# A hybrid encoder trunk: the 96 columns of the small projections become a unit of their own, the gate units get 512 columns

## The chip, the cores and the metric

The kernel runs on one core of one Trainium2 chip. The metric is the device time in microseconds (us) of one execution. Engines are named as the profile names them: PE is TensorE's matmul side and PEld its weight loads, DVE is VectorE, ACT is ScalarE, POOL is GpSimd, SP is SyncE, which issues the transfers.

## The reference

Two layers over 256 tokens of 1024 features, all in float32. What matters here is the input projection of the mixer in the middle of each layer, one matrix of 6752 columns that is cut among all branches:

```python
h = rms_norm(x, mix_norm[l])
z = h @ w_in[l]
(na_q, na_k, na_v, gq, gk, gv, gr, gfl, gbl, c_q, c_kv, k_rope, gates) = split_cols(z, IN_SPLITS)
...
gt = jax.nn.sigmoid(gates.reshape(B, S, N_BRANCH, D))
mixed = (gt[:, :, 0] * (y_na @ w_br_na[l])
         + gt[:, :, 1] * (y_gla @ w_br_gla[l])
         + gt[:, :, 2] * (y_mla @ w_br_mla[l]))
x = x + mixed @ w_out[l]
```

`gates` has 3 x 1024 columns, one set for each branch. Three small parts, `k_rope` (64 columns, the rotary key), `gfl` and `gbl` (16 each, the low-rank decays), have 96 columns together. Around the mixer stand two feed-forward blocks with 2816 inner features.

## The kernel before, in words

The 256 tokens are two tiles of 128 (t = 0, 1). The normalised input lies transposed in `xT`, as the stationary operand of the projections. Every float32 product is made of three matmuls in the type float32r: each operand is split into a high part (hi) and a rest (lo), and `burst` (L372) issues hi x hi, hi x lo and lo x hi for each block k of 128 input features. The product goes through the helper `mm` (L370 in the profile), so the profile has one line for nearly all matmuls, each with a weight load of its own on PEld.

Weights come in *units*, a list (L85 on) in the order of use; a unit is a transfer of up to 128 x 2048 values into one of three `raw` buffers (SP's queue). ACT copies it in two halves to the hi part of an `hl` buffer (L143), DVE subtracts to get the lo part (L149); after the second lo half of unit j the transfer of unit j+3 is issued. `unit()` (L162) hands out the next unit and sees that its halves, and the first of the one after, are in the queues; `tick()` (L186) is called between bursts, splits ahead by up to two units, and moves the side tasks (attention, linear attention) a step on.

`dense8(N, evac)` (L389) is one projection of N columns: two units of four k blocks each, for each unit both token tiles with 12 matmuls of N columns, then the eviction `evac` of each tile's accumulator. So N columns cost 48 matmuls, whatever N is. The order in a mixer is: `m` (latent q and kv), `gr`, then `dense8(512, ev_r)` (L1132), then `v` with the bursts of the unit `uq` (384 columns) between, `q`, `gv`, `k`, the two linear-attention projections, four times `dense8(GATEN, ev_g(g))` (L1162), the two late gate units, the branch products and the output product.

The step with `ev_r` is called the *small-projection step* below. Its 512 columns are the 96 of the small parts and the first 416 of the gates (GATE0). `ev_r` (L622) evicts a tile: DVE scales the 96 columns into `rl` (L624) and copies a part of them (L625), ACT copies the 416 gate columns into `gates` (L627) and sums the squares of 64 columns (L629). The four steps with `ev_g`, the *gate step*, hold the next 4 x 408 gate columns (GATEN), which ACT copies into `gates` (L634). The sigmoid is applied later, in place.

```python
def dense8(N, evac, pre=None, between=None):
    ...
    accs = [acc_t(), acc_t()]
    for kh in range(2):
        u = unit()
        for t in range(2):
            ...
            burst(accs[t][:, :N], X, u, range(4 * kh, 4 * kh + 4), t, N, kh == 0, kh == 1)
```

Of the kernel before, what the change touches and what calls it, by code (L numbers as in the profile page):

```python
# [10 lines left out]
AF = mybir.ActivationFunctionType  # L11
# [7 lines left out]
NCH = DFF // 256  # L19
NB = DFF // 128  # L20
EPS = 1e-6
GATE0 = 416
GATEN = 408

SPLIT_AHEAD = 2
RAW_BUFS = 3
# [20 lines left out]
def body(tc, T):  # L47
# [3 lines left out]
    with ctx:  # L51
# [24 lines left out]
        for l in range(DEPTH):  # L76
            W = T["layers"][l]
            for kh in range(2 if l else 0):
                units.append((W["f1_up"][kh], 2048))
            for c in range(2 if l else 0, NB):  # L80
                units.append((W["f1_w13"][c], 2048))
            for u in range(NCH):
                units.append((W["f1_w2"][u], 2048))
            def add(nm):
                for kh in range(2):  # L85
                    units.append((W["in_" + nm][kh], 2048))

            add("m")
            add("gr")
            add("r")  # L90
            units.append((W["uq"], 1536))
            add("nv")
            add("nq")
            units.append((W["ukv"], 2048))
            add("gv")
            add("nk")
            for j in range(2):
                units.append((W["in_qk"][j], 2048))
            for g in range(4):
                for kh in range(2):  # L100
                    units.append((W["in_g"][g, kh], 4 * GATEN))
            for h in range(2):
                for kh in range(2):
                    units.append((W["in_late"][h, kh], 2048))
            for b in ("na", "mla", "gla"):
                for h in range(2):
                    units.append((W["br_" + b][h], 2048))
            for u in range(4):
                units.append((W["out"][u], 2048))
            for kh in range(2):  # L110
                units.append((W["f2_up"][kh], 2048))
            for c in range(2, NB):
                units.append((W["f2_w13"][c], 2048))
            for u in range(NCH):
                units.append((W["f2_w2"][u], 2048))
# [273 lines left out]
        def dense8(N, evac, pre=None, between=None):  # L389
            tks = []  # L390
            if pre is not None:
                ua, ub = unit(), unit()
                for t in range(2):
                    for h in range(2):
                        finish(pre[t, h])
                    acc = acc_t()
                    burst(acc[:, :N], X, ua, range(4), t, N, True, False)
                    tick(t == 0)
                    burst(acc[:, :N], X, ub, range(4, 8), t, N, False, True)
                    tks.append(drain(evac, t, acc))  # L400
                    tick()
                return tks
# [4 lines that stand above are left out]
                    if kh == 0 and between:  # L407
                        between(t)
                    burst(accs[t][:, :N], X, u, range(4 * kh, 4 * kh + 4), t, N, kh == 0, kh == 1)
                    if kh:  # L410
                        tks.append(drain(evac, t, accs[t]))
                    tick()
            return tks
# [150 lines left out]
        def mixer(l, norms, after, prefetch):  # L564
# [57 lines left out]
            def ev_r(t, acc):  # L622
                r = rl[t] = small(160, tag="rl", bufs=2)
                DVE.tensor_scalar(r[:, :96], acc[:, :96], rs_x[t], None, op0=ALU.mult)  # L624
                DVE.tensor_copy(r[:, 96:].rearrange("p (q n) -> p q n", q=2),  # L625
                                r[:, None, 64:96].to_broadcast([128, 2, 32]))
                ACT.activation(out=gates[:, t, :GATE0], in_=acc[:, 96:512], func=AF.Copy, scale=rs_x[t])  # L627
                ssr[t] = small(1)
                ACT.activation(out=junk(64), in_=r[:, :64], func=AF.Square, accum_out=ssr[t])  # L629

            def ev_g(g):
                def f(t, acc):
                    a = GATE0 + g * GATEN
                    ACT.activation(out=gates[:, t, a:a + GATEN], in_=acc[:, :GATEN], func=AF.Copy, scale=rs_x[t])  # L634
                return f

# [492 lines left out]
            c_tk = spawn(c_task(m_tk), 1)  # L1129
            dense8(512, ev_gr)  # L1130
            rs_bcast()
            dense8(512, ev_r)  # L1132
            prefetch()
            finish(c_tk)
            u_tk = []
# [124 lines left out]
def _tok(a):  # L1260
    return np.ascontiguousarray(a)
# [37 lines left out]
def layout(inp):  # L1299
    A = {}  # L1300
    A["x"] = _tok(inp["x"].reshape(SEQ, D))
    xT = inp["x"].reshape(SEQ, 8, 128).transpose(2, 1, 0)
    A["gcol"] = _tok(inp["ffn1_norm"][0].reshape(8, 128).T)
    A["ident"] = np.eye(128, dtype=np.float32)
    A["rope"] = _rope()
    j, i = np.arange(128)[:, None], np.arange(128)[None, :]
    A["am"] = _tok((j % 64 > i)[:, :64].astype(np.int32))
    dr, dc, ok = _rel_index()
    for l in range(DEPTH):
        p = f"l{l}_"  # L1310
        for f in ("1", "2"):
            w1, w3, w2 = (inp[f"ffn{f}_w{n}"][l] for n in (1, 3, 2))
            a = np.stack([w.reshape(8, 128, NB, 128).transpose(2, 1, 0, 3) for w in (w1, w3)], 3)
            A[p + f"f{f}_w13"] = _tok(a.reshape(NB, 128, 2048))
            if (l, f) == (0, "1"):
                A["first"] = _tok(np.concatenate([xT] + [a[c].reshape(128, 8, 256) for c in range(FIRST_R)], 2))
            else:
                A[p + f"f{f}_up"] = _tok(a[:2].reshape(2, 128, 2, 4, 256).transpose(2, 1, 3, 0, 4).reshape(2, 128, 2048))
            A[p + f"f{f}_w2"] = _kt(w2, 2)
            A[p + f"g{f}"] = _tok(inp[f"ffn{f}_norm"][l].reshape(8, 128).T)  # L1320
        A[p + "gm"] = _tok(inp["mix_norm"][l].reshape(8, 128).T)
        w = inp["w_in"][l]
        sizes = (("nq", 512), ("nk", 512), ("nv", 512), ("gq", 256), ("gk", 256), ("gv", 512), ("gr", 512),
                 ("gfl", 16), ("gbl", 16), ("cq", 256), ("ckv", 256), ("kr", 64), ("gates", 3072))
        part, o = {}, 0
        for nme, n in sizes:
            part[nme] = w[:, o:o + n]
            o += n
        g = part["gates"]
        g = np.concatenate([g[:, :1024], g[:, 2048:], g[:, 1024:2048]], 1)  # L1330
        A[p + "in_gr"] = _k4(part["gr"])
        A[p + "in_m"] = _k4(np.concatenate([part["cq"], part["ckv"]], 1))
        A[p + "in_r"] = _k4(np.concatenate([part["kr"], part["gfl"], part["gbl"], g[:, :GATE0]], 1))
        for nme in ("nq", "nk", "nv", "gv"):
            A[p + "in_" + nme] = _k4(part[nme])
        A[p + "in_qk"] = _tok(np.stack([_kt(part["gq"], 8)[0], _kt(part["gk"], 8)[0]]))
        A[p + "in_g"] = _tok(np.stack([_k4(g[:, GATE0 + i * GATEN:GATE0 + (i + 1) * GATEN]) for i in range(4)]))
        A[p + "in_late"] = _tok(np.stack([_k4(g[:, 2048 + h * 512:2048 + (h + 1) * 512]) for h in range(2)]))
        A[p + "uq"] = _kt(inp["mla_w_uq"][l], 2)[0]
        A[p + "ukv"] = _kt(inp["mla_w_ukv"][l], 2)[0]  # L1340
        for b in ("na", "gla", "mla"):
            wb = inp["w_br_" + b][l]
            A[p + "br_" + b] = _tok(np.stack([_kt(wb[:, h * 512:(h + 1) * 512], 4)[0] for h in range(2)]))
        A[p + "out"] = _kt(inp["w_out"][l], 2)
        A[p + "row"] = np.concatenate([inp["gla_out_norm"][l], inp["mla_q_norm"][l], inp["mla_k_norm"][l],
                                       inp["mla_cq_norm"][l], inp["mla_ckv_norm"][l]])
        col = np.zeros((128, COLN), np.float32)
        col[:, 0] = np.tile(inp["na_q_norm"][l], 2)
        col[:, 1] = np.tile(inp["na_k_norm"][l], 2)
        col[:, 2:4] = inp["gla_gf_bias"][l].reshape(2, 128).T  # L1350
        col[:, 4:6] = inp["gla_gb_bias"][l].reshape(2, 128).T
        A[p + "col"] = col
        gup = np.zeros((32, 512), np.float32)
        gup[:16, :256] = inp["gla_gf_up"][l]
        gup[16:, 256:] = inp["gla_gb_up"][l]
        A[p + "gup"] = gup
        b = np.where(ok[None], inp["na_rpb"][l][:, dr, dc], np.float32(-1e30)).astype(np.float32)
        A[p + "bias"] = _tok(b.reshape(4, 2, 2, 128, 128).transpose(0, 3, 1, 2, 4))
    return A
# [23 lines left out]
```

## Time and profile before

| what | value |
|---|---|
| median of 3 runs | 1239.62 us (1239.03 to 1239.73) |
| the profiled execution | 1239.52 us |
| its span, first to last instruction | 1237.7 us |
| PE busy | 1233.5 us, 100% of the span |
| DVE busy | 892.4 us, 72% |
| ACT busy | 710.9 us, 57% |
| mean granted TensorE clock | 1.000 |

The profile is of one execution, and 1.8 us of its time lie around the span. Matmuls are pipelined: a recorded matmul of 512 columns lasts 0.39 us, while the next one starts 0.23 us after it. A pace is therefore read from a chain or from a row that merges many, and not from the mean of one. A row that merges equal instructions gives the time from the start of the first to the end of the last.

### The profile page before, as it was taken

The numbers are of one execution on the slowest core, as the hardware profiler recorded it, in microseconds if no ns is written. First come the engines' busy times: TensorE is split into PE (matmuls) and PEld (weight loads), VectorE is DVE, ScalarE is ACT, GpSimd is POOL, SyncE is SP. The second block draws the span as 40 slices with busy tenths as digits, with TensorE's granted clock in tenths as the row PEclk, the third lists the DMA queues.
The fourth block names the chain that finished last, engine by engine and source line by source line (L and its number), as shares of the span: only waits on it lengthen the run. The fifth ranks groups of instructions, "written<-read, shape, count | busy, mean of one in ns | idle before, by whom it ended". The sixth has DMA issues, their size and how long they took to land.

```text
span 1237.7 us, 18188 instructions
## 1 busy us (share of the span) xinstructions
PE 1233.5 (100%) x7048; PEld 1061.4 (86%) x7048; DVE 892.4 (72%) x1399; ACT 710.9 (57%) x1317; POOL 217.6 (18%) x165
## 2 busy tenths in 40 slices
PE   9999999999999999999999999999999999999999
PEld 8888888889988888888888888888899888888887
DVE  6888837689667778886478886476896677788862
ACT  7665536567755465655356565356686654656541
POOL 0222102132112012220012220021322030122200
PEclk9999999999999999999999999999999999999999
DMA  8655744662554455557355556346525445555560
GB/s 332 211 202 177 252 150 162 224 195 93 187 190 146 173 200 178 201 177 249 119 204 207 191 195 247 108 172 238 176 99 201 171 142 190 188 195 189 186 238 34
DMA packets 37910, 228.58 MB, mean 185 GB/s; under 512 B 5760, under 2 KB 7040, under 8 KB 13376
## 3 DMA queue, kind: packets, MB, share of 16 engines
q1 hardware_dynamic: 37680, 227.42, 52.0%
q8 instruction: 55, 0.90, 0.3%
q14 instruction: 31, 0.25, 0.1%
q10 hardware_dynamic: 144, 0.00, 0.0%
HBM read 224.26 MB, written 1.05 MB: 182 GB/s over the span
## 4 chain that ended last, share of the span: by engine, by line
PE 100%; DVE 0%; issue 0%
PE acc L370 81%; PE ta L370 16%; PE ta L699 1%; PE ta L264 1%; PE ta L308 0%; PE ta L1211 0%; PE ta L684 0%; PE ta L737 0%; PE ta L616 0%; PE ta L1026 0%; PE ta L299 0%; PE ta L477 0%; PE ta L956 0%; DVE x L554 0%; DVE junk L305 0%
## 5 line engine op out<-in xcount | busy, mean ns | idle before, releaser
L149 DVE TENSOR_TENSOR hl<-raw,hl 128x1024 fp32r<-128x1024 f32 (+1 forms) x418 | 561.2, 1383 | 83.6 <-ACT hl L143 73.2
L143 ACT ACTIVATE hl<-raw 128x1024 fp32r<-128x1024 f32 (+1 forms) x418 | 412.8, 1040 | 103.4 <-PE ta L370 81.3
L370 PE MATMUL acc<-xT,hl 128*128 128x256 f32 (+1 forms) x2720 | 464.7, 332 | 0.0
L370 PEld LDWEIGHTS acc<-xT,hl 128*128 128x128 f32 x2720 | 407.6, 188 | 54.7
L370 PE MATMUL acc<-hl,xT 128*128 128x512 f32 (+1 forms) x1584 | 362.1, 384 | 0.0
L370 PEld LDWEIGHTS acc<-hl,xT 128*128 128x128 f32 x1584 | 291.9, 188 | 47.7 <-issue 1.7
L370 PE MATMUL acc<-hl,s 128*128 128x512 f32 x816 | 193.6, 390 | 0.0
L370 PEld LDWEIGHTS acc<-hl,s 128*128 128x128 f32 x816 | 152.5, 188 | 31.7 <-issue 0.3
L491 POOL TENSOR_TENSOR s<-s,rsb 128x512 f32<-128x512 f32 x79 | 109.5, 1387 | 352.4 <-DVE s L490 352.4
L370 PE MATMUL ta<-hl,s 128*128 128x512 f32 (+2 forms) x648 | 148.3, 378 | 0.0
L370 PEld LDWEIGHTS ta<-hl,s 128*128 128x128 f32 x648 | 117.6, 188 | 21.7
L500 ACT ACTIVATE s<-s 128x256 fp32r<-128x256 f32 x82 | 34.0, 417 | 168.2 <-DVE s L498 168.2
L490 DVE TENSOR_TENSOR s<-acc,s 128x256 f32<-128x256 f32 x158 | 59.7, 420 | 58.4 <-ACT s L489 58.4
L577 POOL TENSOR_TENSOR sm<-sm,mhalf 128x4 f32<-128x4 f32 (+2 forms) x24 | 36.7, 1531 | 192.0 <-DVE sm L581 192.0
L285 POOL TENSOR_TENSOR sm<-sm,mhalf 128x1 f32<-128x1 f32 x12 | 14.1, 1176 | 294.3 <-DVE sm L284 294.3
L489 ACT ACTIVATE s<-acc 128x256 f32<-128x256 f32 x158 | 50.6, 372 | 0.0
L248 DVE TENSOR_TENSOR s<-ta,s 128x512 fp32r<-128x512 f32 (+1 forms) x46 | 26.6, 604 | 30.0 <-ACT s L247 29.9
L267 ACT ACTIVATE xT<-ta,gain 128x128 fp32r<-128x128 f32 x80 | 22.8, 368 | 36.3 <-PE ta L264 36.3
L247 ACT ACTIVATE s<-ta 128x512 fp32r<-128x512 f32 (+1 forms) x46 | 22.9, 532 | 31.4 <-PE ta L699 16.9
L496 ACT ACTIVATE s<-s 128x256 f32<-128x256 f32 x82 | 34.2, 419 | 11.3 <-POOL s L491 0.3
L370 PE MATMUL ta<-s,s 64*64 64x128 f32 (+4 forms) x720 | 35.8, 260 | 0.0
L370 PEld LDWEIGHTS ta<-s,s 64*64 64x64 f32 (+3 forms) x720 | 30.4, 145 | 5.9 <-issue 4.2
(164 smaller groups left out, 676.6 us busy)
## 6 DMA issues: line engine op xcount, KB each, us to landing
raw<-in_l_f_w SPq DMA_DIRECT2D x123, 1024.0 KB, 4.8
raw<-in_l_in_g SPq DMA_DIRECT2D x16, 816.0 KB, 4.4
raw<-in_l_in_late SPq DMA_DIRECT2D x8, 1024.0 KB, 4.8
raw<-in_l_out SPq DMA_DIRECT2D x8, 1024.0 KB, 4.7
raw<-in_l_f_up SPq DMA_DIRECT2D x6, 1024.0 KB, 4.8
raw<-in_l_in_m SPq DMA_DIRECT2D x4, 1024.0 KB, 4.8
raw<-in_l_in_gr SPq DMA_DIRECT2D x4, 1024.0 KB, 4.8
raw<-in_l_in_r SPq DMA_DIRECT2D x4, 1024.0 KB, 4.8
```

Of the source, the lines that this page charges most:

```text
L143: ACT.activation(out=hls[j][:, 0, sl], in_=raws[j][:, sl], func=AF.Copy)
L149: DVE.tensor_tensor(out=hl[:, 1, sl], in0=r[:, sl], in1=hl[:, 0, sl].bitcast(F32), op=ALU.subtract)
L247: ACT.activation(out=hi, in_=ps, func=AF.Copy)
L248: DVE.tensor_tensor(out=lo, in0=ps, in1=hi.bitcast(F32), op=ALU.subtract)
L267: ACT.activation(out=xT[:, t, 0, kk, :], in_=ps[:, k * 128:(k + 1) * 128], func=AF.Copy, scale=G[:, kk:kk + 1])
L370: PE.matmul(out=out, lhsT=lhsT, rhs=rhs, start=start, stop=stop, skip_group_check=True)
L489: ACT.activation(out=g[:, j, :], in_=a[j][:, 256:], func=AF.Copy)
L490: DVE.tensor_tensor(out=g[:, j, :], in0=a[j][:, :256], in1=g[:, j, :], op=ALU.add)
L491: POOL.tensor_tensor(out=g, in0=g, in1=rb[:, None, :].to_broadcast([128, 2, 256]), op=ALU.mult)
L496: ACT.activation(out=g[:, 0, :], in_=g[:, 0, :], func=AF.Silu)
L500: ACT.activation(out=o[:, 0, :], in_=g[:, 0, :], func=AF.Copy)
L577: POOL.tensor_tensor(out=r[:, :n], in0=ss[:, :n], in1=mhalf[:, :n], op=ALU.pow)
```

## The change

The 96 columns get one unit of 768 values a partition (8 blocks of 96), used in one burst of 24 matmuls for each token tile. The first 2048 gate columns come in four steps of 512 columns instead of 416 and 4 x 408. There is one unit fewer in a layer.

```diff
--- before.py
+++ after.py
@@ -19,8 +19,7 @@
 NCH = DFF // 256
 NB = DFF // 128
 EPS = 1e-6
-GATE0 = 416
-GATEN = 408
+GATEN = 512
 
 SPLIT_AHEAD = 2
 RAW_BUFS = 3
@@ -87,7 +86,7 @@
 
             add("m")
             add("gr")
-            add("r")
+            units.append((W["in_r"], 768))
             units.append((W["uq"], 1536))
             add("nv")
             add("nq")
@@ -624,13 +623,12 @@
                 DVE.tensor_scalar(r[:, :96], acc[:, :96], rs_x[t], None, op0=ALU.mult)
                 DVE.tensor_copy(r[:, 96:].rearrange("p (q n) -> p q n", q=2),
                                 r[:, None, 64:96].to_broadcast([128, 2, 32]))
-                ACT.activation(out=gates[:, t, :GATE0], in_=acc[:, 96:512], func=AF.Copy, scale=rs_x[t])
                 ssr[t] = small(1)
                 ACT.activation(out=junk(64), in_=r[:, :64], func=AF.Square, accum_out=ssr[t])
 
             def ev_g(g):
                 def f(t, acc):
-                    a = GATE0 + g * GATEN
+                    a = g * GATEN
                     ACT.activation(out=gates[:, t, a:a + GATEN], in_=acc[:, :GATEN], func=AF.Copy, scale=rs_x[t])
                 return f
 
@@ -1129,7 +1127,12 @@
             c_tk = spawn(c_task(m_tk), 1)
             dense8(512, ev_gr)
             rs_bcast()
-            dense8(512, ev_r)
+            hl = unit()
+            for t in range(2):
+                acc = acc_t()
+                burst(acc[:, :96], X, hl, range(8), t, 96, True, True)
+                ev_r(t, acc)
+                tick()
             prefetch()
             finish(c_tk)
             u_tk = []
@@ -1330,11 +1333,11 @@
         g = np.concatenate([g[:, :1024], g[:, 2048:], g[:, 1024:2048]], 1)
         A[p + "in_gr"] = _k4(part["gr"])
         A[p + "in_m"] = _k4(np.concatenate([part["cq"], part["ckv"]], 1))
-        A[p + "in_r"] = _k4(np.concatenate([part["kr"], part["gfl"], part["gbl"], g[:, :GATE0]], 1))
+        A[p + "in_r"] = _kt(np.concatenate([part["kr"], part["gfl"], part["gbl"]], 1), 8)[0]
         for nme in ("nq", "nk", "nv", "gv"):
             A[p + "in_" + nme] = _k4(part[nme])
         A[p + "in_qk"] = _tok(np.stack([_kt(part["gq"], 8)[0], _kt(part["gk"], 8)[0]]))
-        A[p + "in_g"] = _tok(np.stack([_k4(g[:, GATE0 + i * GATEN:GATE0 + (i + 1) * GATEN]) for i in range(4)]))
+        A[p + "in_g"] = _tok(np.stack([_k4(g[:, i * GATEN:(i + 1) * GATEN]) for i in range(4)]))
         A[p + "in_late"] = _tok(np.stack([_k4(g[:, 2048 + h * 512:2048 + (h + 1) * 512]) for h in range(2)]))
         A[p + "uq"] = _kt(inp["mla_w_uq"][l], 2)[0]
         A[p + "ukv"] = _kt(inp["mla_w_ukv"][l], 2)[0]
```

On PE, in the first layer, at the small-projection step (`acc` is its accumulator, `hl` the split weights, `s` and `xT` stationary operands, `ta` the other accumulators; a row gives the columns and how many follow each other). Before:

```order
L616 MATMUL ta<-idt,s_1898 128x128 x2
L616 MATMUL ta<-idt,s_1939 128x128 x2
L370 MATMUL acc<-hl,xT 128x512 x12
L299 MATMUL ta<-idt,sm 128x128 x2
L370 MATMUL acc<-hl,xT 128x512 x48
L370 MATMUL ta<-hl,s_1963 128x384 x2
L370 MATMUL ta<-hl,s_1964 128x384
L370 MATMUL ta<-hl,s_1963 128x384 x2
```

and in the changed kernel:

```order
L615 MATMUL ta<-idt,s_1898 128x128 x2
L615 MATMUL ta<-idt,s_1939 128x128 x2
L369 MATMUL acc<-hl,xT 128x512 x12
L298 MATMUL ta<-idt,sm 128x128 x2
L369 MATMUL acc<-hl,xT 128x96 x48
L369 MATMUL ta<-hl,s_1963 128x384 x2
L369 MATMUL ta<-hl,s_1964 128x384
L369 MATMUL ta<-hl,s_1963 128x384 x2
```

Nothing moves; the 48 matmuls have 96 columns in place of 512, and the 12 of `uq` that follow are the same.

On ACT, from the splits of the small-projection weights to those of the weights of `v` (`hl<-raw` are the hi halves; between them L247 splits the transposed latents, L586 evicts `gr`, `gates<-acc` is L627). Before:

```order
L143 ACTIVATE hl<-raw 128x1024 x2
L247 ACTIVATE s_1963<-ta 128x512
L586 ACTIVATE s_1979<-acc,sm 128x512
L143 ACTIVATE hl<-raw 128x1024 x2
L247 ACTIVATE s_1990<-ta 128x512
L586 ACTIVATE s_2006<-acc,sm 128x512
L301 ACTIVATE rsb<-ta 128x256
L143 ACTIVATE hl<-raw 128x768 x2
L627 ACTIVATE gates<-acc,sm 128x416
L629 ACTIVATE junk,sm<-rl 128x64
L143 ACTIVATE hl<-raw 128x1024 x2
L627 ACTIVATE gates<-acc,sm 128x416
```

and in the changed kernel:

```order
L142 ACTIVATE hl<-raw 128x384 x2
L246 ACTIVATE s_1963<-ta 128x512
L585 ACTIVATE s_1979<-acc,sm 128x512
L142 ACTIVATE hl<-raw 128x768 x2
L246 ACTIVATE s_1990<-ta 128x512
L585 ACTIVATE s_2006<-acc,sm 128x512
L300 ACTIVATE rsb<-ta 128x256
L627 ACTIVATE junk,sm<-rl 128x64
L142 ACTIVATE hl<-raw 128x1024 x2
L627 ACTIVATE junk,sm<-rl 128x64
```

The two halves of the second unit and the two copies into `gates` are gone, the halves of the first are 384 columns wide, and those of `uq` (768) stand one place earlier.

On DVE, the lo halves around the evictions of line 624 (623 in the changed kernel). Before:

```order
L149 TENSOR_TENSOR hl<-raw,hl 128x1024 x2
L248 TENSOR_TENSOR s_1964<-ta,s_1963 128x512
L248 TENSOR_TENSOR s_1991<-ta,s_1990 128x512
L149 TENSOR_TENSOR hl<-raw,hl 128x1024 x2
L149 TENSOR_TENSOR hl<-raw,hl 128x768 x2
L624 TENSOR_SCALAR rl<-acc,sm 128x96
L625 COPY rl<-rl 128x64
L624 TENSOR_SCALAR rl<-acc,sm 128x96
L625 COPY rl<-rl 128x64
L149 TENSOR_TENSOR hl<-raw,hl 128x1024 x3
```

and in the changed kernel:

```order
L148 TENSOR_TENSOR hl<-raw,hl 128x384 x2
L247 TENSOR_TENSOR s_1964<-ta,s_1963 128x512
L247 TENSOR_TENSOR s_1991<-ta,s_1990 128x512
L148 TENSOR_TENSOR hl<-raw,hl 128x768 x2
L623 TENSOR_SCALAR rl<-acc,sm 128x96
L624 COPY rl<-rl 128x64
L623 TENSOR_SCALAR rl<-acc,sm 128x96
L624 COPY rl<-rl 128x64
L148 TENSOR_TENSOR hl<-raw,hl 128x1024 x3
```

Two lo halves are gone; the evictions of both tiles stand ahead of the three lo halves of the next weights in both.

## Rows read from the trace of the kernel before

**Rows 1.** The page, busy time and share by engine; the chain that ended last.

```profile
PE 1233.5 (100%) x7048; PEld 1061.4 (86%) x7048; DVE 892.4 (72%) x1399; ACT 710.9 (57%) x1317; POOL 217.6 (18%) x165
...
PE 100%; DVE 0%; issue 0%
PE acc L370 81%; PE ta L370 16%; PE ta L699 1%; PE ta L264 1%; PE ta L308 0%; PE ta L1211 0%; PE ta L684 0%; PE ta L737 0%; PE ta L616 0%; PE ta L1026 0%; PE ta L299 0%; PE ta L477 0%; PE ta L956 0%; DVE x L554 0%; DVE junk L305 0%
```

**Rows 2.** The view of who waits for whom, PE: total us, times, longest.

```profile
PE ta L308 <- DVE junk L305: 1.2, 1, 1.2
```

**Rows 3.** The chain in order of time: start us, us, what, how many.

```profile
214.12 10.91 PE acc L370 x48
225.03 2.10 PE ta L370 x12
...
282.70 2.88 PE acc L370 x24
...
301.16 4.47 PE acc L370 x24
...
307.95 4.48 PE acc L370 x24
...
316.69 4.67 PE acc L370 x24
...
828.88 10.91 PE acc L370 x48
...
915.93 4.47 PE acc L370 x24
```

**Rows 4.** Busy time by stretch: small-projection step, then gate step, layer 0.

```profile
core 0: us, PE busy (x) PEld busy (x) DVE busy (x) ACT busy (x) POOL busy (x), PEclk, DMA share, GB/s
213.90:224.90 11.00, 11.00 (x51) 9.10 (x50) 6.31 (x7) 4.63 (x9) 2.12 (x1) 1.00 0.51 183
...
300.90:348.40 47.50, 47.50 (x372) 44.83 (x370) 33.90 (x80) 31.80 (x73) 9.63 (x8) 1.00 0.51 179
```

**Rows 5.** Groups of line 370 in the small-projection step: count, busy us, mean ns, idle.

```profile
L370 PE MATMUL acc<-hl,xT 128*128 128x512 f32 x48 | 11.2, 391 | 0.0
L370 PEld LDWEIGHTS acc<-hl,xT 128*128 128x128 f32 x48 | 8.9, 188 | 1.8
```

**Rows 6.** Weight loads from 316.60 to 316.75 us, in order of time.

```profile
316.62 0.30 PEld L370 LDWEIGHTS acc<-hl,xT 128*128 128x128 f32 x2 [0.17 <-issue]
```

**Rows 7.** PE around 282 us in order of time; the same transposes as a group.

```profile
281.67 1.03 PE L699 MATMUL ta<-idt,s 128*128 128x128 f32 x8
...
L699 PE MATMUL ta<-idt,s 128*128 128x128 f32 x96 | 13.3, 275 | 0.0
```

**Rows 8.** The lo halves of line 149 by shape, VectorE.

```profile
L149 DVE TENSOR_TENSOR hl<-raw,hl 128x1024 fp32r<-128x1024 f32 x382 | 527.1, 1420 | 83.6 <-ACT hl L143 73.2
...
L149 DVE TENSOR_TENSOR hl<-raw,hl 128x816 fp32r<-128x816 f32 x32 | 30.7, 1001 | 0.0
```

**Rows 9.** DMA issues: count, KB each, median us to landing.

```profile
raw<-in_l_in_g SPq DMA_DIRECT2D x16, 816.0 KB, 4.4
...
raw<-in_l_in_r SPq DMA_DIRECT2D x4, 1024.0 KB, 4.8
```

**Rows 10.** VectorE, ScalarE and PE from 221 to 228 us, in order of time.

```profile
222.35 0.32 DVE L624 TENSOR_SCALAR rl<-acc,sm 128x96 f32<-128x96 f32 x1 [2.65 <-PE acc L370]
...
225.07 0.32 DVE L624 TENSOR_SCALAR rl<-acc,sm 128x96 f32<-128x96 f32 x1 [2.17 <-PE acc L370]
...
225.53 3.49 DVE L149 TENSOR_TENSOR hl<-raw,hl 128x1024 fp32r<-128x1024 f32 x3
...
222.70 0.61 ACT L627 ACTIVATE gates<-acc,sm 128x416 f32<-128x416 f32 x1 [6.27 <-DVE rl L624]
...
223.45 1.99 ACT L143 ACTIVATE hl<-raw 128x1024 fp32r<-128x1024 f32 x2
225.42 0.61 ACT L627 ACTIVATE gates<-acc,sm 128x416 f32<-128x416 f32 x1
...
224.87 2.27 PE L370 MATMUL ta<-hl,s 128*128 128x384 f32 x12
226.97 1.31 PE L370 MATMUL acc<-hl,xT 128*128 128x512 f32 x5
```

## The prediction

> **What bounds the kernel now.** I read the page first. TensorE (PE) is busy for the whole span, and the chain of waits that ends last is PE for 100% of it, nearly all of it the matmuls of line 370 [rows 1]. Then the view of who waits for whom: PE waited once, for 1.2 us at the start [rows 2]. The reader is to see that no transfer, eviction or weight split holds PE anywhere. So the time of this kernel is the sum of the paces of its matmuls, and a change is worth what it does to them, unless it uncovers a new wait. Third, the chain in order of time [rows 3], from which a pace is a piece's time divided by its count: 48 matmuls of 512 columns in 10.91 us are 0.2273 us each, 24 of 408 in 4.47 are 0.1863, 24 of 256 in 2.88 are 0.1200. The same pieces of layer 1 have the same times. A piece of 24 that comes after a group of small products reads 4.67, a start cost that has nothing to do with its columns.
>
> Two things follow. The step from 256 to 512 columns costs 0.1073 us, 0.00042 us a column, and what is left over at no columns is 0.0127 us. And by that line 408 columns should take 0.1837; they take 0.0026 more. PE is at a granted clock of 1.00, the level of 2.4 GHz, in both stages that change [rows 4].
>
> **The change, part by part.** Per layer the small-projection step had 48 matmuls of 512 columns and keeps 48, of 96. The gate step had 192 of 408 and keeps 192, of 512. Matmuls, weight loads and columns (48 x 416 fewer, 192 x 104 more, both 19,968) stay equal. Only the paces decide.
>
> *Gate step.* 192 x (0.2273 - 0.1863) = **+7.87 us** a layer [rows 3]. The price is sure, since the small-projection step runs 512 columns of the same two operands now [rows 5].
>
> *Small-projection step, removed.* **-10.91 us** a layer, the chain's piece for it [rows 3].
>
> *Small-projection step, added.* No matmul of the float32r type with fewer than 256 columns runs in this kernel, so the pace at 96 is not in the trace and is bounded. From below: if a matmul costs by its columns, the line above gives 0.0127 + 96 x 0.00042 = 0.053. But each of these matmuls also has a weight load of 128 columns. A load is recorded at 0.188 us [rows 5]; at the start of a burst two of them follow each other with no matmul done between, and the two together last 0.30 us [rows 6], so the second starts 0.11 us after the first. That is how fast loads can follow each other. At 512, 408 or 256 columns the matmul is about as long as a load or longer and covers it; a matmul of 96 columns, 0.040 us of columns, covers less than half of one. So the load sets the pace: 0.110. A little above stands 0.120, the pace at 256 columns, if a load costs a matmul there its last 0.01 us. From above: if load and matmul come one after the other, 0.110 + 0.053 = 0.163. I take 0.110, from the row that measures this very load; it lies between the ends. A nearby row says the same with another type: eight transposes of 128 columns, each with a load of its own, last 1.03 us together and 0.27 alone, 0.109 from one to the next [rows 7]. So 48 x 0.110 = **+5.28 us** a layer (2.54 and 7.82 at the ends).
>
> Here two rules speak for the ends. The Trainium skill, "TensorE: Matmul & The Clock Gate", section "Back-to-back issue gap", prices an isolated matmul at N/2.4 + 2.5 ns, by columns alone; by it 96 columns are 42.5 ns (an estimate from that page), and with equal columns and counts both kernels take the same time. The trace does not quite agree: 0.2273 us at 512 columns where the rule has 0.216. The same page, Part 3, "The mechanism", says that a weight load overlaps matmuls in flight only when it goes to another row group of the array. By it every matmul here, on all 128 rows, would pay its load in full; the trace speaks against it, with 0.1200 us for a 256-column matmul and its load together.
>
> *Sum.* 7.87 - 10.91 + 5.28 = +2.24 us a layer, **+4.5 us** for two. Against the profiled execution's own time of 1239.52 us that is 1244.0; the median of the runs shown is 0.1 above it, so I say 1244.1. With 0.120 it would be +5.4.
>
> *What costs nothing.* In the gate step each split of a unit into hi and lo grows from 816 to 1024 columns, on VectorE from 1.00 to at most 1.42 us [rows 8], 16 a layer, 6.7 us more; VectorE is busy 33.9 of 47.5 us there [rows 4] and PE's stage grows by 7.9, so it stays behind PE. ScalarE, at 31.8 of 47.5, gains less. The transfers grow from 816 to 1024 KB, 4.4 to 4.8 us to landing [rows 9], for a unit that PE now uses up in 5.45 us instead of 4.47. The two gate copies of line 627 leave ScalarE, 0.61 us each [rows 10]; it was not the bound.
>
> *What is late next.* VectorE's queue has the evictions of both token tiles (line 624) ahead of the lo halves of the next weights (nv). In the trace the second eviction begins at 225.07, the lo halves at 225.53, the first of three is done about 1.2 us later, and PE wants it at 226.97, after 12 matmuls of uq [rows 10]. In the changed kernel this order stays, the uq burst stays between, and what remains is the same 0.2 to 0.3 us of spare. ScalarE's hi halves of nv start after the first eviction, which now comes 24 short matmuls, 2.64 us, before the second instead of 2.7 [rows 10], so they do not become later either. The transfers gain: r brings 384 KB where two units of 1024 stood, and nv is issued one unit earlier.
>
> **The rivals.**
> 1. *Columns alone set the pace* (the side that is not slower). The weight loads stay hidden at 96 columns, since loads are pulled ahead while matmuls run. For it: at 256 columns a load recorded at 0.188 hides in a pace of 0.120, so loads do overlap in part. Against: the two loads of [rows 6] were held back by nothing the profile shows and still stood 0.11 apart. Price: 0.053, 48 x 0.053 = 2.54, net 7.87 - 10.91 + 2.54 = -0.50 a layer, 1238.6. It decides below 0.089 us a matmul, where the sum falls under +2.5 us, which is 0.2%, about what a measurement of this kernel can tell from no change.
> 2. *Load, then matmul.* A short matmul has no room for the next load, and the pace is the sum, 0.163: 7.82 - 10.91 + 7.87 = +4.78 a layer, 1249.2. For it: each pace above carries 0.0127 us that no column explains. Against: 256 columns at 0.120, where a sum would be 0.22.
> 3. *A wait behind the short step.* If the spare of 0.2 to 0.3 us is used up, PE waits for a lo half of nv, at most one half of 1.2 us a layer: +2.4 on top, 1246.5. For it: the spare is thin. Against: no instruction is put between, and PE never waited there.
>
> **How the numbers follow.** The forecast (load-bound, 0.105 to 0.125, 1243.6 to 1245.5) has 0.62; rival 1 0.14, rival 2 0.15, rival 3 0.07; 0.02 is left for what I do not see. The range reaches from 1241.0 (a pace of 0.08, some of the load hidden) up over rivals 3 and 2 to 1250.0, and leaves out most of rival 1. Rival 1 is the case within 0.2%: 0.14 for the same. Faster by over 0.2% would need a gain that no row shows, the 0.02. The forecast and rivals 2 and 3 are slower by more: 0.84.
>
> **What would show it.** In the chain of the changed kernel: a piece of 48 for the small projections of 5.3 us a layer (2.5 if rival 1 holds, 7.8 if rival 2), starts of weight loads 0.11 apart there, gate pieces of 24 at 5.45 us, and still no wait of PE beyond 1.2 us. I am wrong if PE waits for VectorE or a transfer in the 20 us after the step, if the gate step's 512 columns take another pace than 0.227, or if the granted clock falls below 1.00 in a step whose matmuls keep the array less than half filled with columns.

## The result, and the profile after

| | before | changed |
|---|---|---|
| median | 1239.03 us (1238.82 to 1239.73, 5 executions) | 1247.66 us (1244.51 to 1251.44, 5 executions) |
| the profiled execution | 1239.52 us | 1247.66 us |
| its span | 1237.7 us | 1245.9 us |
| its mean granted TensorE clock | 1.000 | 0.997 |

The ratio is 1.0066, with a 95% interval of 1.0052 to 1.0080: slower by 0.7%. The five executions differ more than those before: they took 1247.66, 1251.44, 1244.56, 1248.92 and 1244.51 us, and their mean granted clocks were 0.997, 0.994, 1.000, 0.996 and 1.000. The two with a whole clock are at 1244.5, where the forecast was 1244.1; the others lost part of the clock and are 3 to 7 us longer.

The page of the changed kernel, its head, the busy times, the chain that ended last, and the two costliest groups:

```profile
span 1245.9 us, 18177 instructions
...
PE 1241.5 (100%) x7048; PEld 1057.3 (85%) x7048; DVE 891.2 (72%) x1395; ACT 710.7 (57%) x1309; POOL 216.5 (17%) x165
...
PE 100%; DVE 0%; issue 0%
...
L148 DVE TENSOR_TENSOR hl<-raw,hl 128x1024 fp32r<-128x1024 f32 (+1 forms) x414 | 560.4, 1394 | 85.4 <-ACT hl L142 75.0
L142 ACT ACTIVATE hl<-raw 128x1024 fp32r<-128x1024 f32 (+1 forms) x414 | 412.3, 1048 | 103.9 <-PE ta L369 81.3
```

PE is still the whole chain [rows 1], and 8 us longer. VectorE is not busier than before. The view of who waits for whom, for PE:

```profile
PE ta L307 <- DVE junk L304: 1.2, 1, 1.2
```

It is the same 1.2 us at the start as before [rows 2]: no new wait. So the paces changed, and they stand in the chain in order of time (start us, us, what, how many):

```profile
213.97 5.29 PE acc L369 x48
219.27 2.17 PE ta L369 x12
221.44 2.76 PE acc L369 x12
...
303.24 5.47 PE acc L369 x24
...
313.49 5.65 PE acc L369 x24
...
831.21 6.72 PE acc L369 x48
837.92 3.91 PE ta L369 x12
841.84 2.76 PE acc L369 x12
```

In layer 0 the 48 matmuls of 96 columns took 5.29 us where 48 of 512 took 10.91 [rows 3]. The pieces of 24 in the gate step shown here take 5.47 and 5.65 where they took 4.47 and 4.67 [rows 3]. In layer 1, at 831.21, the same 48 matmuls took 6.72 us, and the 12 of `uq` behind them 3.91 instead of 2.17. What happened between shows in the busy times by stretch (the columns after POOL are the granted clock, the DMA share and GB/s):

```profile
core 0: us, PE busy (x) PEld busy (x) DVE busy (x) ACT busy (x) POOL busy (x), PEclk, DMA share, GB/s
831.20:834.70 3.50, 3.50 (x35) 3.50 (x33) 3.29 (x5) 1.16 (x5) 1.40 (x1) 1.00 0.02 5
834.90:841.60 6.70, 6.70 (x27) 6.70 (x27) 3.61 (x5) 4.36 (x7) 0.00 (x0) 0.50 0.44 157
841.70:850.00 8.30, 8.30 (x41) 7.16 (x40) 5.65 (x14) 6.69 (x20) 2.41 (x2) 1.00 0.74 254
```

From 834.9 to 841.6 us PE was granted half of its clock, the lower of its two levels, 1.2 GHz. Before that stretch it had issued short matmuls for 3.5 us; on both sides of it the clock is whole. The two pieces lost (6.72 - 5.29) + (3.91 - 2.17) = 3.17 us, which is the distance of this execution from those with a whole clock, 1247.66 - 1244.5. The Trainium skill ("TensorE: Matmul & The Clock Gate", Part 1) describes the half clock as the default of an idle array, and the full one as what activity releases. The rows agree with the two levels; but PE was not idle here, it was busy for 3.50 of the 3.50 us before the fall and for all 6.70 us of it.

The weight loads of the step in layer 0, as the timeline merges them:

```profile
213.70 5.44 PEld L369 LDWEIGHTS acc<-hl,xT 128*128 128x128 f32 x48
```

48 loads in 5.44 us, of which the last alone is 0.19 [rows 5]: (5.44 - 0.19) / 47 = 0.1117 us from one to the next, the matmuls' own pace of 5.29 / 48 = 0.110. PE's loads follow each other without a break and the matmuls keep their pace; that they wait for the loads is tested below. The place behind the step, on VectorE, where the prediction saw little to spare, came out as forecast:

```profile
219.31 0.32 DVE L623 TENSOR_SCALAR rl<-acc,sm 128x96 f32<-128x96 f32 x1 [2.01 <-PE acc L369]
...
219.77 3.49 DVE L148 TENSOR_TENSOR hl<-raw,hl 128x1024 fp32r<-128x1024 f32 x3
```

The lo halves of the next weights start 0.46 us after the second eviction, as in [rows 10]. The first is done 1.2 us later, at about 221.0, and PE wants it at 221.3 or later: 0.3 us to spare, and PE waited for none of them.

### The profile page after: what moved, and what is told of

It is laid out like the page before. It is cut to its first block, busy times and chain, and to the rows that moved or that the text cites. A ratio compares the mean times of both kernels' runs of the same rounds, so it can differ in the third digit from the quotient of the medians.

```text
span 1245.9 us, 18177 instructions
## 1 busy us (share of the span) xinstructions
PE 1241.5 (100%) x7048; PEld 1057.3 (85%) x7048; DVE 891.2 (72%) x1395; ACT 710.7 (57%) x1309; POOL 216.5 (17%) x165
## 4 chain that ended last, share of the span: by engine, by line
PE 100%; DVE 0%; issue 0%
PE acc L369 81%; PE ta L369 16%; PE ta L697 1%; PE ta L263 1%; PE ta L307 0%; PE ta L735 0%; PE ta L1214 0%; PE ta L682 0%; PE ta L298 0%; PE ta L1024 0%; PE ta L615 0%; PE ta L476 0%; PE ta L954 0%; DVE x L553 0%; DVE junk L304 0%
## 5 line engine op out<-in xcount | busy, mean ns | idle before, releaser
L369 PE MATMUL acc<-hl,xT 128*128 128x512 f32 (+1 forms) x1584 | 368.4, 388 | 0.0
L369 PEld LDWEIGHTS acc<-hl,xT 128*128 128x128 f32 x1584 | 287.1, 189 | 57.9 <-issue 1.7
L247 DVE TENSOR_TENSOR s<-ta,s 128x512 fp32r<-128x512 f32 (+1 forms) x46 | 26.6, 604 | 34.5 <-ACT s L246 34.4
```

What stands on the lines that cost most here:

```text
L247: DVE.tensor_tensor(out=lo, in0=ps, in1=hi.bitcast(F32), op=ALU.subtract)
L369: PE.matmul(out=out, lhsT=lhsT, rhs=rhs, start=start, stop=stop, skip_group_check=True)
```

## The experiments

One theory was set against two rivals. *Theory L*: a float32r matmul with a load of its own takes 0.0127 us and 0.00042 us a column, but never less than its load, 0.112 (the expectations write 0.1115); and the run of short matmuls lets the clock fall in some executions. *Rival K*: the columns set the pace. *Rival C*: the falls are chance and have nothing to do with the change. Each ratio is against executions of the kernel before that ran beside it (medians 1239.25 to 1239.36).

### The changed kernel again

No edit.

> The changed kernel itself, for more executions. Theory L (the weight load sets the pace of a 96-column matmul, 0.112 us each, and the 5.3 us in which the array is filled with columns for about a third of the time let the granted clock fall in some executions): executions with a mean clock of 1.000 at 1244.5 us, those with a fall at 1247.6 or more, nothing between. Rival C (the falls are chance and have nothing to do with the change): executions of the kernel before show falls as often.

Measured: 1249.24 us (1248.67 to 1250.05, 4 executions), ratio 1.0081 (1.0067 to 1.0094), clocks of 0.996, 0.994, 0.996 and 0.996. No execution of the kernel before that ran beside it had a clock other than 1.000. The profiled one, busy times by stretch (the clock is the third number from the end):

```profile
214.00:218.30 4.30, 4.30 (x41) 4.30 (x41) 3.27 (x5) 1.96 (x5) 1.40 (x1) 1.00 0.14 21
218.30:225.10 6.80, 6.80 (x25) 6.51 (x25) 3.92 (x5) 5.66 (x14) 0.00 (x0) 0.50 0.50 177
225.10:240.00 14.90, 14.90 (x69) 12.64 (x68) 10.22 (x24) 7.72 (x17) 2.92 (x2) 1.00 0.75 265
834.00:839.50 5.50, 5.50 (x52) 5.50 (x50) 3.63 (x5) 2.93 (x6) 1.40 (x1) 1.00 0.22 42
839.60:843.00 3.40, 3.40 (x12) 3.40 (x12) 3.29 (x5) 2.42 (x5) 0.00 (x0) 0.50 0.54 217
```

Here the clock fell in both layers, each time while or just after the short matmuls ran, and for different lengths: 6.8 us in layer 0 and 3.4 in layer 1. With the first five, two of nine executions kept a whole clock. The expectation had those with a fall at 1247.6 or more, which holds. The kernel before shows no falls, so rival C is out as it was put; the next runs tell whether the short matmuls are what the falls go with.

### The step padded to 256 columns

```diff
-            units.append((W["in_r"], 768))
+            units.append((W["in_r"], 2048))
-                burst(acc[:, :96], X, hl, range(8), t, 96, True, True)
+                burst(acc[:, :256], X, hl, range(8), t, 256, True, True)
...
```

The layout appends 160 gate columns to the 96.

> The small-projection unit is padded to 256 columns (160 gate columns computed twice and not used), same 48 matmuls and 48 loads a layer. Theory L: a matmul costs its load at 96 columns and 0.120 us at 256, so only 48 x 0.008 us a layer more, 1245.3 us with the clock whole; and as the array is filled now, no falls, all executions within 0.5 us. Rival K (columns set the pace): 160 columns more cost 48 x 0.067 us a layer, 6.4 us above the changed kernel. Rival C (falls are chance): falls as in the changed kernel.

Measured: 1245.30 us (1244.73 to 1245.74, 5 executions), ratio 1.0047 (1.0034 to 1.0061), all clocks 1.000. The chain at the step:

```profile
214.09 5.75 PE acc L369 x48
219.84 2.08 PE ta L369 x12
```

160 more columns cost 5.75 - 5.29 = 0.46 us a layer, a hundredth of a microsecond for each matmul, where K wanted 3.2 us. With wider matmuls in the same place and number, the clock stayed whole in all five. The padded kernel does more work than the changed one, and its median is 2.4 us below that of the changed kernel's first five executions.

### Two halves of 48 columns

```diff
-                burst(acc[:, :96], X, hl, range(8), t, 96, True, True)
+                for c in range(2):
+                    o = acc[:, c * 48:c * 48 + 48]
+                    for k in range(8):
+                        a = k * 96 + c * 48
+                        mm(o, X(0, k, t), hl[:, 0, a:a + 48], k == 0 and c == 0, False)
+                        mm(o, X(0, k, t), hl[:, 1, a:a + 48], False, False)
+                        mm(o, X(1, k, t), hl[:, 0, a:a + 48], False, k == 7)
```

> The 96 columns in two halves of 48: 96 matmuls and loads a layer for the same columns. Theory L: 48 x 0.1115 = 5.35 us a layer more, 1255.2 us with the clock whole; 10.7 us of an array filled for under a fifth of the time, so a fall in both layers of every execution, 3 us or more each: 1261 to 1268. Rival K (columns set the pace, 0.0127 us a matmul on top): 48 x 0.0127 = 0.6 us a layer more, 1245.7. Rival C: falls no oftener than in the changed kernel.

Measured: 1271.03 us (1270.71 to 1271.76, 4 executions), ratio 1.0257 (1.0243 to 1.0271), clocks of 0.986 and 0.987, outside the 1261 to 1268 of the expectation. The chain's piece for the step in layer 0, and the busy times by stretch around it:

```profile
213.88 17.13 PE acc L369 x96
```

```profile
213.90:217.20 3.30, 3.30 (x31) 3.30 (x32) 2.83 (x3) 0.82 (x2) 1.40 (x1) 1.00 0.00 0
217.30:234.20 16.90, 16.90 (x76) 16.90 (x76) 3.64 (x7) 4.99 (x9) 0.00 (x0) 0.50 0.18 63
234.40:240.00 5.60, 5.60 (x29) 5.02 (x29) 4.25 (x10) 3.92 (x16) 1.91 (x1) 1.00 0.74 236
```

The direction is that of theory L, far from K's 1245.7; the size expected was too small. The clock fell in both layers, as expected, but for 17 us each time, and at half of the clock the loads stand about twice as far apart: after some 31 matmuls in the first 3.3 us of the step, the other 65 took 13.8 us, 0.21 each. The step took 17.13 us in place of the 10.7 that 96 loads at 0.112 make. So a fall lengthens the stretch of short matmuls in which it came.

### The short matmuls spread among wide ones

The weights of the step leave the units. In the second half of `gr`, six matmuls of 96 columns follow each three of 512:

```diff
...
+                        for i in range(4):
+                            burst(accs[t], X, u, [4 + i], t, 512, False, i == 3, i)
+                            for k in (2 * i, 2 * i + 1):
+                                hi, lo = (w[:, k % 4 * 96:k % 4 * 96 + 96] for w in rs[k // 4])
+                                mm(acc[:, :96], X(0, k, t), hi, k == 0, False)
+                                mm(acc[:, :96], X(0, k, t), lo, False, False)
+                                mm(acc[:, :96], X(1, k, t), hi, False, k == 7)
...
```

> The same 48 matmuls of 96 columns a layer, but spread in groups of six among the 512-column matmuls of the step before (gr), with their weights split apart from the units. Theory L: the load prices stay, 1244.5 us, and as no stretch of low fill is left, no falls: all executions within 0.5 us of it and a clock of 1.000. If the falls come from the number of short matmuls wherever they stand, or by chance, they stay, 1247.6 and more in some executions.

Measured: 1245.30 us (1244.81 to 1245.61, 5 executions), ratio 1.0048 (1.0035 to 1.0060), all clocks 1.000. PE's waits:

```profile
PE ta L308 <- DVE junk L305: 1.2, 1, 1.2
PE acc L370 <- DVE hl L147: 0.4, 2, 0.2
```

The same number of matmuls and loads, and no fall in five executions, beside seven in nine where they stand together. 0.4 us of the 0.8 above 1244.5 are waits for a lo half that the new order uncovers; the rest is open. So the falls go not with the number of short matmuls but with their standing together.

### One load for two products

```diff
...
+                o = acc[:, :192].rearrange("p (w n) -> p w n", w=2)
+                for k in range(8):
+                    a = k * 96
+                    mm(o, X(0, k, t), hl[:, :, a:a + 96], k == 0, False)
+                    mm(acc[:, :96], X(1, k, t), hl[:, 0, a:a + 96], False, k == 7)
...
```

The eviction adds the columns 96 to 191 to the first 96; for that ScalarE first copies them out (`low`, L624), and VectorE adds (L625).

> Hi x hi and hi x lo share one load: one matmul of 192 columns (hi and lo weights side by side) and one of 96 for each block, 32 matmuls and loads a layer instead of 48 for the same columns; the two halves are added when evicted. Theory L: 16 loads of 0.1115 us fewer, -1.78 us a layer, 1241.0 us with the clock whole; the array is filled for more than half of the time, so falls are rarer or gone. Rival K (columns set the pace): 16 x 0.0127 us a layer fewer, 0.4 us in all, 1244.1.

Measured: 1244.19 us (1243.97 to 1244.62, 5 executions), ratio 1.0041 (1.0028 to 1.0053), all clocks 1.000. Alone, this number is K's. PE's waits and its timeline in layer 0 say otherwise:

```profile
PE acc L369 <- DVE hl L148: 3.0, 2, 1.5
PE ta L307 <- DVE junk L304: 1.2, 1, 1.2
```

```profile
213.38 3.75 PE L369 MATMUL acc<-hl,xT 128*128 128x192 f32 x32
216.97 2.31 PE L369 MATMUL ta<-hl,s 128*128 128x384 f32 x12
219.13 0.40 PE L369 MATMUL acc<-hl,xT 128*128 128x512 f32 x1
221.00 1.20 PE L369 MATMUL acc<-hl,xT 128*128 128x512 f32 x4 [1.48 <-DVE hl L148]
```

32 matmuls in about 3.6 us are loads at 0.11 us, but PE waited 1.48 us for the lo half of the next weights behind it. It is the wait of the prediction's rival 3: the evictions of both tiles stand ahead of the lo halves. Not only the shorter step brought it about, but also the longer eviction. Its copy on ScalarE stood behind two hi halves:

```profile
217.02 1.99 ACT L142 ACTIVATE hl<-raw 128x1024 fp32r<-128x1024 f32 x2
218.92 0.32 ACT L624 ACTIVATE low<-acc,sm 128x96 f32<-128x96 f32 x1
219.27 0.32 DVE L625 SCALAR_TENSOR_TENSOR rl<-acc,sm,low 128x96 f32<-128x96 f32 x1 [2.31 <-ACT low L624]
```

So VectorE began the second eviction 2.3 us after PE had gone on to `uq` (216.97); in the changed kernel it began 0.04 us after (219.31 and 219.27). The next run places the splits of the next unit ahead of the evictions:

```diff
...
             hl = unit()
+            fill()
...
+                while t == 0 and st["lo"] < st["hi"]:
+                    emit_lo()
                 ev_r(t, acc)
...
```

> The shared load again, with the splits of the next unit ahead of the evictions in ScalarE's and VectorE's queues. Theory L with the wait: the 3.0 us of PE's waits for lo halves go, and the 32 loads of 0.1115 us stay: 1241.0 us, clock whole. If the loads set no price and the 3.0 us belong to the step, it stays at 1244.2.

Measured: 1241.04 us (1240.42 to 1241.47, 11 executions), ratio 1.0013 (1.0004 to 1.0022), all clocks 1.000. PE's waits, and the chain at the step:

```profile
PE ta L307 <- DVE junk L304: 1.2, 1, 1.2
```

```profile
213.69 3.51 PE acc L369 x32
217.20 2.15 PE ta L369 x12
```

The wait is gone, and 16 loads fewer a layer for the same columns took 3.5 us off the changed kernel's 1244.5. K is out.

No run takes the load from a short matmul and leaves the rest, so these runs price the two together, at 0.11 us. That the load sets this price rests on the two loads that stand 0.11 us apart with no matmul done between [rows 6], and on a piece of the chain of the kernel before, in the attention:

```profile
332.75 1.21 PE ta L370 x32
```

These are 32 matmuls in plain float32 on parts of the array, each with a load of only 64 columns, and they take 0.038 us each. So a matmul with a load of its own does not cost 0.11 us as such.

### The gate part alone

The gate step keeps 512 columns; the small-projection step goes back to two units of 512, of which 416 columns are gates computed twice.

```diff
-            units.append((W["in_r"], 768))
+            add("r")
...
+            dense8(512, ev_r)
...
```

> The gate part alone: the gate step has 512 columns as in the changed kernel, and the small-projection step keeps 512 columns in two units as before (416 gate columns computed there a second time and not used). All theories that take paces from the chain: 192 x 0.0410 us a layer more than the kernel before, 15.7 us, 1255.0, no falls. If the wider gate units uncover a wait (transfer or split), it is more than that.

Measured: 1254.95 us (1254.87 to 1255.13, 4 executions), ratio 1.0128 (1.0112 to 1.0143), all clocks 1.000. 15.7 us above the kernel before, 7.85 a layer. In the chain the pieces of the gate step are those of the changed kernel:

```profile
300.49 5.47 PE acc L369 x24
...
308.27 5.47 PE acc L369 x24
...
318.51 5.65 PE acc L369 x24
```

### Swapped operands

The 96 weight columns become the stationary operand and the tokens move; for each block one matmul of 512 columns (hi and lo of both tiles) and one of 256. Two transposes bring the result back.

```diff
...
+            acc = acc_t()
+            o = acc[:96, :].rearrange("p (w t n) -> p w t n", w=2, t=2)
+            for k in range(8):
+                a = k * 96
+                mm(o, hl[:, 0, a:a + 96], xT[:, :, :, k, :].rearrange("p t w n -> p w t n"), k == 0, False)
+                mm(o[:, 0], hl[:, 1, a:a + 96], xT[:, :, 0, k, :], False, k == 7)
+            r_tk = run(r_task(acc))
...
```

> The small projections with the operands swapped: the 96 weight columns are stationary, the tokens move, per block one matmul of 512 columns (hi and lo of both tiles) and one of 256, 16 matmuls a layer; two transposes bring the result back. Theory L: 8 x (0.2273 + 0.1170) + 0.22 = 2.97 us a layer for the step, so 7.87 - 10.91 + 2.97 = -0.07 a layer against the kernel before: 1239.2 us, no falls, level with the kernel before. If the transposes and evictions hold PE, up to 1 us a layer more.

Measured: 1252.35 us (1251.62 to 1253.54, 4 executions), ratio 1.0107 (1.0094 to 1.0121), clocks of 0.997 and 0.994. That is far from the expected 1239.2; the next run shows that the order is to blame and not the step. PE's waits:

```profile
PE ta L636 <- DVE s L825: 8.5, 2, 4.3
PE ta L307 <- DVE junk L304: 1.2, 1, 1.2
```

The transposes (L636) stood behind two `uq` bursts and waited 4.3 us in each layer for the eviction of a `uq` burst (L825), which frees the accumulator bank that they need. The clock was below 1.000 in all four executions; in the profiled one it fell right behind that wait, at 228.3 us:

```profile
224.00:228.20 4.20, 0.26 (x3) 0.29 (x4) 3.74 (x10) 1.37 (x3) 1.91 (x1) 1.00 0.36 84
228.30:231.60 3.30, 3.30 (x9) 2.56 (x9) 2.37 (x7) 1.28 (x7) 0.00 (x0) 0.50 0.70 246
```

So a wait of PE can cost the clock too, and short matmuls are not the only way to it. The mended order puts them behind the first `uq` burst, in a bank of the other group (`acc`), and the splits of the next unit ahead:

```diff
-                yield 4
-                ps = tr_t()
+                yield 3
+                ps = acc_t()
...
+            fill()
...
+            step(r_tk)
...
```

> The swapped operands again, with the order mended: the weight splits of the next unit stand ahead in the queues, the two transposes come right behind the first uq burst and use an accumulator bank. Theory L: 2.81 us for the 16 matmuls (as read from the first swapped kernel) and 0.22 for the transposes in place of 10.91, and 7.85 more in the gate step (half of what the gate part alone cost): -0.03 us a layer against the kernel before, 1239.2 us, with the clock whole and no wait of PE over 1.2 us. If the waits of the first swapped kernel come from the swapping itself and not from the order, 1247 to 1252.

Measured: 1239.51 us (1239.10 to 1239.97, 11 executions), ratio 1.0001 (0.9992 to 1.0009), all clocks 1.000. The chain at the step (L636 are the transposes):

```profile
213.51 2.80 PE acc L369 x16
216.31 2.08 PE ta L369 x12
218.40 0.17 PE acc L636 x2
```

The two parts of the mending were not run apart. This kernel has the gate units of the change and none of its loss: it is level with the kernel before, not ahead of it.

### The same columns cut otherwise

The kernel before with 480 columns in the first step and 4 x 416 in the gate step.

```diff
-GATE0 = 416
-GATEN = 408
+GATE0 = 384
+GATEN = 416
...
```

> The kernel before with its columns cut otherwise: 96 + 384 = 480 in the small-projection step, 4 x 416 in the gate step. If 416 columns lie on the line of the wide matmuls (0.0127 + 0.000419 N, 0.1870 us) and the 0.0026 us that 408 takes above it is gone: 48 x 0.2138 + 192 x 0.1870 = 46.2 us a layer against 46.7, 1238.3 us. If that excess belongs to the step and not to the width: 1239.3, no change.

Measured: 1239.66 us (1238.99 to 1240.89, 11 executions), ratio 1.0004 (0.9996 to 1.0013): no change. The chain's pieces, 480 columns and then 416:

```profile
213.83 10.49 PE acc L370 x48
...
300.44 4.54 PE acc L370 x24
```

416 columns take 4.54 / 24 = 0.1892 us, 0.0022 above the line of theory L, and 480 columns, in the other step, 10.49 / 48 = 0.2185, 0.0047 above it. So the 0.0026 us of [rows 3] belong neither to the width of 408 nor to the gate step: 408, 416 and 480 columns all lie above the line through 256 and 512, and why stays open.

## Why the prediction was right, and where it was short

The time lies in the range and on the forecast side. For an execution with a whole clock the mechanism is the forecast one. That the median is in the range as well is partly luck: 1247.66 lies above the forecast's own band of 1243.6 to 1245.5, in the part that was there for rivals 2 and 3. Neither of them came; a loss of the clock, which had no term, put it there. Point by point:

- *Gate step, +7.87 us a layer.* Right: 7.85 where it was done alone, and the chain's seven whole pieces of 24 in a layer are 0.98 to 1.04 longer each.
- *Small-projection step, 5.28 us in place of 10.91.* Right, and for the reason given: 5.29 us, loads 0.1117 us apart. Padding to 256 columns at 0.46 us a layer shows that columns are not what is paid for, and 16 loads a layer fewer at a gain of 3.5 us that loads with their matmuls are. Rival 1 (columns alone) is out by its own mark, 2.5 us for the step; so is rival 2 (load and matmul one after the other, 7.8).
- *The sum, 1244.1.* Right for an execution with a whole clock, 1244.5, which is 5.2 above the 1239.3 of the kernel before. The terms as measured make 2 x (7.85 - 10.91 + 5.29) = 4.5; the other 0.7 us are in none of them, and no run looked for them.
- *Cover behind the step.* Right: no wait in the changed kernel. It was as thin as said; the shared load, with a step 1.8 us shorter and a longer eviction, fell through it for 1.5 us a layer.
- *The clock.* Here the prediction was short, and wrong by its own last sign: it named a granted clock below 1.00 in this step as what would show it wrong, but gave it no term and no rival, so that it fell under the 0.02 for the unseen. It came in seven of nine executions, and is worth 3.2 us in the profiled one, some two thirds of the forecast sum again. Of the 3.6 us by which the median, 1247.66, is above the number, these are 3.2. With a little more of it the range would have failed: one of the first five executions took 1251.44 us, above its end at 1250.0. The kernel before could have warned only by what it lacks: it has no float32r matmul below 256 columns, so none of its rows shows what a run of them does to the clock.

## What to carry to other kernels

A matmul that brings its own weight load is paid for by the load as soon as its columns no longer cover it; here that was 0.11 us for a load of 128 columns, which 96 moving columns cost and 256 hardly more. So a cut that keeps columns and matmuls equal is not neutral when one piece falls below some 256 columns. Cut evenly, or share a load among products, or swap the operands so that the narrow side is the stationary one. And where short matmuls must be, put wide ones among them: standing together they cost the clock in most executions here, which shows first as a spread of the times.

## What the runs showed of the hardware

- The granted clock fell to half with PE busy throughout (3.50 of 3.50 us before the fall, 6.70 of 6.70 in it). With 48 matmuls of 96 columns together it was below 1.000 in seven of nine executions, in the profiled ones in stretches of 3.4 to 6.8 us that began during them or just behind; with 96 of 48 columns in all four, in the profiled one for 17 us in each layer. It stayed whole with 48 of 256 columns (5 executions), with 32 of 192 and 96 columns (16), and with the 96-column ones spread among wide ones (5). It also fell once PE had waited 4.3 us, in the first kernel with swapped operands. What decides between a whole and a fallen clock for the same program was not settled.
- A weight load's distance from the next about doubled with the half clock: 65 of 48 columns in 13.8 us are 0.21 each, where 0.112 is the distance at the whole clock.
- Loads overlap matmuls on the same 128 rows of the array: 256 columns and a load together take 0.1200 us [rows 3], where one load behind another takes 0.1117 and the columns alone 0.107 (an estimate, 256 x 0.00042).
